# Pairs of heads on alternating halves of the array, zero-padded rotary keys, and a scaling moved to GpSimd, in the attentions of a two-block kernel

## The chip, the cores and the metric

The kernel runs on one core of a Trainium2 chip, as one launch. The metric is the device time of the launch in microseconds (us), here the median of several runs. Engine names are those of the profile: PE is TensorE's matmul side and PEld its weight load, DVE is VectorE, ACT is ScalarE, POOL is GpSimd, SP is SyncE, which issues the DMAs.

## What is computed

A token matrix x of 256 rows and 1024 features goes through two blocks of two layers each. The first block (feed-forward, a three-branch mixer, attention to a memory, feed-forward) is left alone by the change. The second block works on x and on a context of 256 more rows. Its layer 0 ("even") has two attentions side by side, a differential and a latent one, for x and for the context; its layer 1 ("odd") has one attention of 16 heads for x alone. Cut to these:

```python
def diff_attend(q, k, v, lam, lam_init, out_g):      # 4 heads, each with two 64-wide q/k parts i
    s = jnp.einsum('bhiqd,bhikd->bhiqk', q, k) * (DA_DK ** -0.5)
    p = softmax_f32(s)
    a = p[:, :, 0] - lam * p[:, :, 1]
    o = jnp.einsum('bhqk,bhkd->bhqd', a.astype(v.dtype), v)
    return rms_norm_2(o, out_g) * (1.0 - lam_init)

def mla_attend(qn, qr, kn, kr, v):                   # 4 heads: 128 plain + 64 rotary, kr shared
    s = (jnp.einsum('bhqd,bhkd->bhqk', qn, kn) + jnp.einsum('bhqd,bkd->bhqk', qr, kr)) * ((MLA_NOPE + MLA_ROPE) ** -0.5)
    p = softmax_f32(s)
    return jnp.einsum('bhqk,bhkd->bhqd', p.astype(v.dtype), v)

def na_latent(q, k, v, kc, vc, rpb):                 # 16 heads of 64, keys of x and of the context
...
        s_loc = jnp.einsum('bhqd,bhiwd->bhqiw', q_row, kb).astype(jnp.float32) * scale + bias
...
        p = softmax_f32(jnp.concatenate([s_loc, s_ctx], axis=-1))
...
```

## The kernel before, in words

Weight products, most of the program, go in three float32r passes (L241 to L243), their weights split on ACT (L236) and DVE (L237). A scheduler sets each engine's order from the traced program, the tile pools and the dependencies. Scores take a bank of the PSUM pool pj (four banks); transposes and values take one of the pool pa (four).

**Even layer.** `even_project` makes the operands; `latent_block` is called four times (two streams, two token blocks) and leaves the rotary keys `krT` on 128 rows. For each of the four heads the same 64 rotary keys serve, so both halves of the 128 rows hold them. `attend` runs units (a head and a token block of 128 queries) as a pipeline by `skew`: the scores and softmax of a unit, then its transposes (L316, copy L1309), then its values, each a stage behind the other. In `latent_attend` a unit's scores are, for each of one or two key streams, a product over 128 rows (L1239) and one over 64 rows (L1240) on the half `b` of the head. In `diff_attend` a unit has two score banks, part i = 0 on rows 0 to 63 and i = 1 on rows 64 to 127, one after the other (L1276). The context's attentions (eight units each) have 256 keys, x's have 512. Adaln weight products (L924) fill in at `fill`.

**Odd layer.** `odd_attend` has 32 units, one head h and one token block tb each. A unit: two score products over 64 rows (L1369), the bias added in PSUM on DVE (L1372), row maximum (L496), its negative (L497), the exponential with its sum on ACT (L499), the reciprocal (L501), the scaling of the 128x512 weights on DVE (L506), four transposes (L316), their copy on ACT (L1382), four value products into 64 columns of the head pair's bank (L1392). After a pair's last unit the pair's 128x256 output is split (L236, L237). The bias of a head comes from a table loaded by two DMAs from `rpbF` into a k2 tile and added to a mask on POOL (L1364), once per head. The k2 pool has seven tiles; a load waits for the tile's last reader.

The softmax's statistics `mx` and `sm` come from rings of four tiles. `fill("odd")` has nothing left to trace, as the adaln filler has ended before.

Of the kernel before, what the change touches and what calls it, by code (L numbers as in the profile page):

```python
# [35 lines left out]
# The steps take y = s y0 to 8192 s^27 v^-0.5; the seed is the negative, by its sign bit.  # L36
# [4 lines left out]
# Units of filler by the place where they are traced, a digit for each visit of it.  # L41
# [8 lines left out]
class Split:  # L50
    """Feature-major activations [128, n, 256], as an exact sum of two float32r parts."""
# [11 lines left out]
    def put(self, net, i, c, y):  # L63
        """Columns c of the features 4 i to 4 i + 3."""
        net.split(self.hs[i][:, :, c], self.ls[i][:, :, c], y)


class Joint:
    """Two streams' Splits of 1024 features in common tiles, for products with both at once."""
# [13 lines left out]
class Stream:  # L83
    """One stream of a Joint, as a Split."""
# [17 lines left out]
class Weights:  # L102
    """One loaded unit of weights as float32r parts, held in two tiles."""
# [11 lines left out]
class Net:  # L115
# [19 lines left out]
    # ---------------------------------------------------------------- tiles  # L135
# [37 lines left out]
    # -------------------------------------------------------------- weights  # L173
    def weight(self, src, n, amid=None):
        half = n // 2 if n > UNIT // 2 else n
        parts = []
        for o in range(0, n, half):
# [9 lines left out]
            if amid:  # L187
                # the first of all: by quarters, what it is for between them
# [35 lines left out]
    def fill(self, place):  # L224
        """Trace as much of the filler as belongs to this visit of a place."""
# [3 lines left out]
    def until(self, thirds):  # L229
        """Bring the adaln filler past that many thirds, and on to where it holds no bank."""  # L230
# [14 lines left out]
    def colsA(self, ps, w, base, step, xs):  # L245
        """ps [cols, 256] = (weight columns)^T x over the 1024 features."""
# [5 lines left out]
    def pair(self, src, xs):  # L252
        """Two column tiles of 128 in one bank."""
# [6 lines left out]
    def groupB(self, src, width, streams, major=False, between=None, fill=None):  # L260
        """Token-major projections of 1024 features: (stream, token block, bank) in turn."""
# [106 lines left out]
    def post_ln(self, acc, x, scale, l, i, eps, want_xs=True):  # L368
        """x = LN(scale * x + acc), in place, for the four accumulators acc[tb][nh]."""
# [15 lines left out]
    # ------------------------------------------------------------------ ffn  # L385
# [1246 lines left out]
```

## Time and profile before

| | |
|---|---|
| median of 3 runs | 2645.27 us (2642.64 to 2647.34) |
| span of the profiled execution | 2638.9 us |
| PE busy | 2581.5 us, 98% |
| DVE busy | 1495.0 us, 57% |
| ACT busy | 1176.3 us, 45% |
| POOL busy | 43.2 us, 2% |
| share of PE in the chain that ended last | 87% |
| even attentions, first L1239 to last L1253 | 1646.0 to 1767.4 us |
| odd attention, first L1369 to last L1392 | 2324.5 to 2411.6 us |

The span runs from the first to the last instruction of the profiled execution; the time of a run is taken from outside and holds a little more. "Busy" is the time in which an engine executes; the two last rows of the table are stretches of the same span, read from the timeline.

### The profile page before, as it was taken

The page shows a single profiled execution, that of the slowest core. Times are in us where ns is not written, and L with a number is a line of the kernel's source. Part 1 is how long each engine was busy: PE and PEld are TensorE (multiplying, and loading weights), DVE is VectorE, ACT ScalarE, POOL GpSimd, SP SyncE. Part 2 cuts the span into 40 slices and gives each one's busy share as a digit, 9 for nine tenths or more (in the row PEclk, how much of TensorE's full clock was granted, in tenths as well). Part 3 has the DMA queues.
Part 4 walks back from the last instruction along what each step waited for, and adds up shares of the span by engine and source line. Part 5 has one row for each costly group of instructions (what it writes and reads, how often), then busy time and mean ns, then how long its engine had stood idle before and what let it go on. Part 6 is the DMA issues. An engine that isn't in the chain of part 4 may idle for free.

```text
span 2638.9 us, 40347 instructions
## 1 busy us (share of the span) xinstructions
PE 2581.5 (98%) x15946; PEld 2178.1 (83%) x15946; DVE 1495.0 (57%) x3006; ACT 1176.3 (45%) x1953; POOL 43.2 (2%) x52
## 2 busy tenths in 40 slices
PE   8999999999999999999999999999999999999999
PEld 7997789969979978799699776567888776777997
DVE  5546765665456557655664757656222337555554
ACT  5444454554444444544544545444222325444443
POOL 0000100000000001000000000000000000010000
PEclk9999999999999999999999999899999999999999
DMA  7565335655556555256565542424222435432453
GB/s 256 189 216 191 133 112 181 200 204 206 189 179 208 197 173 204 90 168 205 203 223 191 184 152 80 140 102 150 104 96 96 161 106 186 121 72 64 169 192 136
DMA packets 136493, 424.19 MB, mean 161 GB/s; under 512 B 29752, under 2 KB 32480, under 8 KB 136304
## 3 DMA queue, kind: packets, MB, share of 16 engines
q1 hardware_dynamic: 136304, 421.62, 47.2%
q8 instruction: 125, 2.05, 0.3%
q14 instruction: 64, 0.52, 0.1%
HBM read 417.33 MB, written 4.24 MB: 160 GB/s over the span
## 4 chain that ended last, share of the span: by engine, by line
PE 87%; DVE 5%; DMA 4%; ACT 2%; issue 1%; SPq 0%; POOL 0%; ACTq 0%; DVEq 0%; POOLq 0%
PE pj L241 17%; PE pj L242 17%; PE pj L243 17%; PE pa L242 7%; PE pa L241 7%; PE pa L243 7%; PE pa L316 3%; PE pj L924 2%; DMA wf<-in_ffn_w_inA_dram 2%; PE pa L1392 1%; DVE wl L237 1%; DMA wa<-in_mod_wB_dram 1%; PE pj L1369 1%; DMA wf<-in_mix_A_dram 1%; PE pj L1276 1%
## 5 line engine op out<-in xcount | busy, mean ns | idle before, releaser
L237 DVE TENSOR_TENSOR wl<-wf,wh 128x1024 fp32r<-128x1024 f32 (+1 forms) x652 | 785.1, 1205 | 740.2 <-ACT wh L236 735.6
L236 ACT CAST wh<-wf 128x1024 fp32r<-128x1024 f32 (+1 forms) x652 | 670.6, 1032 | 929.9 <-PE pj L242 425.9
L241 PE MATMUL pj<-k,wh 128*128 128x256 f32 (+2 forms) x2896 | 841.7, 291 | 2.1 <-ACT k L236 2.1
L242 PE MATMUL pj<-k,wh 128*128 128x256 f32 (+2 forms) x2896 | 839.9, 290 | 0.0
L243 PE MATMUL pj<-k,wl 128*128 128x256 f32 (+2 forms) x2896 | 839.8, 290 | 0.0
L241 PEld LDWEIGHTS pj<-k,wh 128*128 128x128 f32 (+1 forms) x2896 | 555.3, 192 | 17.3 <-issue 7.0
L243 PEld LDWEIGHTS pj<-k,wl 128*128 128x128 f32 (+1 forms) x2896 | 555.0, 192 | 10.7 <-issue 3.4
L242 PEld LDWEIGHTS pj<-k,wh 128*128 128x128 f32 (+1 forms) x2896 | 555.0, 192 | 10.5 <-issue 3.2
L242 PE MATMUL pa<-wl,k 128*128 128x512 f32 x688 | 274.0, 398 | 0.0
L241 PE MATMUL pa<-wh,k 128*128 128x512 f32 x688 | 272.0, 395 | 0.0
L241 PE MATMUL pj<-wh,k 128*128 128x512 f32 (+1 forms) x616 | 247.8, 404 | 12.2 <-ACT wh L236 7.0
L242 PE MATMUL pj<-wl,k 128*128 128x512 f32 (+1 forms) x616 | 247.3, 402 | 0.0
L243 PE MATMUL pa<-wh,a 128*128 128x512 f32 x560 | 218.1, 389 | 0.0
L243 PE MATMUL pj<-wh,k 128*128 128x512 f32 (+1 forms) x496 | 198.5, 401 | 0.2 <-DVE k L237 0.2
L241 PEld LDWEIGHTS pj<-wh,k 128*128 128x128 f32 x616 | 117.4, 191 | 49.2 <-issue 8.3
L241 PEld LDWEIGHTS pa<-wh,k 128*128 128x128 f32 x688 | 128.8, 187 | 33.5 <-issue 0.8
L242 PEld LDWEIGHTS pa<-wl,k 128*128 128x128 f32 x688 | 129.2, 188 | 28.6 <-issue 1.0
L242 PEld LDWEIGHTS pj<-wl,k 128*128 128x128 f32 x616 | 117.3, 190 | 29.8 <-DVE wl L237 2.3
L236 ACT CAST k<-k 128x512 fp32r<-128x512 f32 (+2 forms) x152 | 85.7, 578 | 106.3 <-PE pa L242 39.0
L243 PEld LDWEIGHTS pa<-wh,a 128*128 128x128 f32 x560 | 105.3, 188 | 25.5 <-issue 0.4
L243 PEld LDWEIGHTS pj<-wh,k 128*128 128x128 f32 x496 | 94.9, 191 | 23.5 <-DVE jc L326 2.1
L237 DVE TENSOR_TENSOR a<-k,k 128x512 fp32r<-128x512 f32 x85 | 57.8, 687 | 50.4 <-ACT k L236 50.4
(252 smaller groups left out, 2523.4 us busy)
## 6 DMA issues: line engine op xcount, KB each, us to landing
wf<-in_ffn_w_inA_dram SPq DMA_DIRECT2D x262, 512.0 KB, 3.7
wf<-in_ffn_w_outB_dram SPq DMA_DIRECT2D x132, 512.0 KB, 3.8
wf<-in_mix_A_dram SPq DMA_DIRECT2D x108, 512.0 KB, 3.7
wa<-in_mod_wB_dram SPq DMA_DIRECT2D x96, 512.0 KB, 4.2
wf<-in_w_branchA_dram SPq DMA_DIRECT2D x32, 384.0 KB, 3.2
wf<-in_od_w_dram SPq DMA_DIRECT2D x24, 512.0 KB, 4.7
wf<-in_w_mix_outB_dram SPq DMA_DIRECT2D x16, 512.0 KB, 3.9
wf<-in_w_outB_dram SPq DMA_DIRECT2D x16, 512.0 KB, 7.9
```

The costliest lines, as they stand in the source:

```text
L236: self.nc.scalar.copy(h, x)
L237: self.nc.vector.tensor_tensor(l, x, h.bitcast(F32), ALU.subtract)
L241: mm(ps, sh, mh, start=start, stop=False)
L242: mm(ps, sh, ml, start=False, stop=False)
L243: mm(ps, sl, mh, start=False, stop=stop)
L316: self.nc.tensor.transpose(ps[:, i * P:(i + 1) * P], b, self.ident)
L924: mm(ps[32 * c:32 * c + 32, :256], self.cond[:, k], w[:, c * 256:c * 256 + 256], start=k == 0, stop=k == KT - 1)
L1276: mm(ps[:, j * T:(j + 1) * T], q["dqT"][b, h, c], k["dkT"][b, h], start=True, stop=True)
L1369: mm(ps[:, j * T:(j + 1) * T], q["qT"][hp // 4][b, hp % 4, c], k["kT"][hp // 4][b, hp % 4], start=True, stop=True)
L1392: mm(po[hp][b, c], kv[n // 2]["v"][n % 2][:, h * 64:h * 64 + 64], pT[:, n * P:(n + 1) * P], start=n == 0, stop=n == 3)
```

## The change

1. `latent_block` copies the rotary keys into two 128-row matrices, rows 0 to 63 of the one and rows 64 to 127 of the other; the rest is zero from two POOL memsets per stream. The rotary product of `latent_attend` is then over all 128 rows, with the matrix of the head's parity.
2. `diff_attend` takes both banks first, and issues the two parts' products alternately.
3. `attend` has one more stage, which does nothing, between the weights and their transposes.
4. `odd_attend` has units of a pair of heads and a token block, 16 of them. The two heads' scores alternate between the halves of the rows, the value products between the halves of the columns; the weights of both heads lie in one k4 tile; the scaling is a POOL instruction; a pair's biases are issued a pair ahead; there is the same empty stage; `fill("odd")` is gone.

```diff
@@ latent_block @@
-        A.copy(o["krT"][:, c], pt[:, 384:])
+        for i in range(2):
+            b = slice(64 * i, 64 * i + 64)
+            A.copy(o["krT"][b, i, c], pt[b, 384:])
@@ even_project @@
-            lat.append({"krT": self.k1(), "qnT": self.four(), "qrT": self.k2().rearrange("p (c t) -> p c t", c=2),
+            lat.append({"krT": self.t([P, 512], "sc", 2).rearrange("p (h t) -> p h t", h=2), "qnT": self.four(), "qrT": self.k2().rearrange("p (c t) -> p c t", c=2),
+            for i in range(2):
+                self.nc.gpsimd.memset(lat[s]["krT"][64 - 64 * i:128 - 64 * i, i], 0.0)
@@ latent_attend @@
-                mm(ps[:, j * T:(j + 1) * T], q["qrT"][b, h // 2, c], k["krT"][b], start=False, stop=True)
+                mm(ps[:, j * T:(j + 1) * T], q["qrT"][:, h // 2, c], k["krT"][:, h % 2], start=False, stop=True)
@@ diff_attend @@
+            banks = [self.pj() for _ in range(2)]
+            for j, k in enumerate(kv):
+                for i in range(2):
+                    b = slice(64 * i, 64 * i + 64)
+                    mm(banks[i][:, j * T:(j + 1) * T], q["dqT"][b, h, c], k["dkT"][b, h], start=True, stop=True)
             for i in range(2):
-                b = slice(64 * i, 64 * i + 64)
-                ps = self.pj()
-                for j, k in enumerate(kv):
-                    mm(ps[:, j * T:(j + 1) * T], q["dqT"][b, h, c], k["dkT"][b, h], start=True, stop=True)
@@ attend @@
-        self.skew(units, lambda u, nb, w, v, n, _: w(*u), turned, lambda u, nb, w, v, n, p: v(*u, p),
-                  lambda *_: None, lambda u, nb, w, v, n, _: n and n(*u))
+        self.skew(units, lambda u, nb, w, v, n, _: w(*u), lambda u, nb, w, v, n, p: p, turned,
+                  lambda u, nb, w, v, n, p: v(*u, p), lambda *_: None, lambda u, nb, w, v, n, _: n and n(*u))
@@ odd_attend @@
+        def weights(hp, tb, _):
+            if hp == 0 and tb == 0:
+                biases(0)
             c = slice(tb * P, (tb + 1) * P)
-            ps = self.pj()
+            banks = [self.pj() for _ in range(2)]
             for j, k in enumerate(kv):
-                mm(ps[:, j * T:(j + 1) * T], q["qT"][hp // 4][b, hp % 4, c], k["kT"][hp // 4][b, hp % 4],
-                   start=True, stop=True)
+                for i in range(2):
+                    b = slice(64 * i, 64 * i + 64)
+                    mm(banks[i][:, j * T:(j + 1) * T], q["qT"][hp // 4][b, hp % 4, c], k["kT"][hp // 4][b, hp % 4],
+                       start=True, stop=True)
             e0 = (2 - 2 * tb) * 64
-            V.tensor_tensor(ps[:, :T], ps[:, :T], bias[h][:, e0:e0 + T], ALU.add)
-            p = self.a2()
-            sm = self.softmax(ps, [(0, 512)], 1.0, p)
-            self.scale_groups(p, [(0, 512)], sm)
-            self.fill("odd")
+            p = self.k4()
+            for i in range(2):
+                ps = banks[i]
+                V.tensor_tensor(ps[:, :T], ps[:, :T], bias[2 * hp + i][:, e0:e0 + T], ALU.add)
+                pi = p[:, i * 512:i * 512 + 512]
+                sm = self.softmax(ps, [(0, 512)], 1.0, pi)
+                nc.gpsimd.tensor_scalar(pi, pi, sm[:, 0:1], 1.0, ALU.mult, ALU.mult)
+            if tb == 0 and hp < 7:
+                biases(hp + 1)
             return p
...
+            for n in range(4):
+                for i in range(2):
+                    h = 2 * hp + i
+                    mm(po[hp][64 * i:64 * i + 64, c], kv[n // 2]["v"][n % 2][:, h * 64:h * 64 + 64],
+                       pT[i][:, n * P:(n + 1) * P], start=n == 0, stop=n == 3)
...
+        self.skew([(hp, tb) for hp in range(8) for tb in range(NT)], weights, lambda hp, tb, p: p, turned, values)
```

The diff alone doesn't show the order that results. Names below are tiles with their numbers; a left side of 64x128 or 128x256 is the shape that one product writes. On PE, in the middle of the odd attention, the order before is, for some three units of one head:

```order
L1369 MATMUL pj_23115<-k_4240_21803,k_4146_21464 128x256
L1369 MATMUL pj_23143<-k_4238_21801,k_4146_21464 128x256
L1369 MATMUL pj_23143<-k_4240_21803,k_4146_21464 128x256
L316 MATMUL pa_23103<-ident,a_4549_23065 128x128 x4
L1392 MATMUL pa_23110<-a_4553_23078,k_4385_22364 64x128
L1392 MATMUL pa_23110<-a_4553_23078,k_4386_22365 64x128
L1392 MATMUL pa_23110<-a_4553_23078,k_4387_22366 64x128
L1392 MATMUL pa_23110<-a_4553_23078,k_4388_22367 64x128
L1392 MATMUL pa_23110<-a_4561_23108,k_4385_22364 64x128
```

And now, for one unit of a pair of heads (the transposes belong to the unit two before, the values to the one three before):

```order
L1379 MATMUL pj_22854<-k_4237_21808,k_4145_21471 128x256
L1379 MATMUL pj_22855<-k_4237_21808,k_4145_21471 128x256
L1379 MATMUL pj_22854<-k_4239_21810,k_4145_21471 128x256
L1379 MATMUL pj_22855<-k_4239_21810,k_4145_21471 128x256
L316 MATMUL pa_22877<-ident,k_4465_22757 128x128 x4
L316 MATMUL pa_22884<-ident,k_4465_22757 128x128 x4
L1408 MATMUL pa_22891<-a_4487_22835,k_4385_22372 64x128
L1408 MATMUL pa_22891<-a_4489_22842,k_4385_22372 64x128
L1408 MATMUL pa_22891<-a_4487_22835,k_4386_22373 64x128
```

The products of one shape stand together now, four score products of two banks by turns, then eight transposes, then eight value products of two turned tiles (two of each `a` tile's four products are seen).

On DVE, the odd attention's steady order (a unit of tb = 1, behind the reciprocals of the unit of tb = 0):

```order
L501 RECIPROCAL sm_22909<-sm_22909 128x1
L1385 TENSOR_TENSOR pj_22957<-pj_22957,k_4483_22823 128x256
L501 RECIPROCAL sm_22917<-sm_22917 128x1
L237 TENSOR_TENSOR k_4423_22634<-pa_22891,k_4421_22632 128x256
L496 TENSOR_REDUCE mx_22965<-pj_22957 128x1
L1385 TENSOR_TENSOR pj_22958<-pj_22958,k_4485_22828 128x256
L497 TENSOR_SCALAR mx_22965<-mx_22965 128x1
L496 TENSOR_REDUCE mx_22973<-pj_22958 128x1
L497 TENSOR_SCALAR mx_22973<-mx_22973 128x1
L501 RECIPROCAL sm_22966<-sm_22966 128x1
L501 RECIPROCAL sm_22974<-sm_22974 128x1
```

The scaling is gone from this engine; each unit's first bias addition stands next to the reciprocals of the unit before, which wait for ACT's sums.

On POOL, which in this stage had only the 16 bias additions, six of them now come first (heads 0 to 5), then the scalings of units 0 and 1, and then:

```order
L1367 TENSOR_TENSOR k_4483_22823<-k_4482_22820,a_4425_22636 128x384
L1388 TENSOR_SCALAR k_4450_22710<-k_4450_22710,sm_22713 128x512
L1388 TENSOR_SCALAR k_4450_22710<-k_4450_22710,sm_22721 128x512
L1388 TENSOR_SCALAR k_4465_22757<-k_4465_22757,sm_22760 128x512
L1388 TENSOR_SCALAR k_4465_22757<-k_4465_22757,sm_22768 128x512
L1367 TENSOR_TENSOR k_4485_22828<-k_4484_22825,a_4425_22636 128x384
L1388 TENSOR_SCALAR k_4477_22803<-k_4477_22803,sm_22806 128x512
L1388 TENSOR_SCALAR k_4477_22803<-k_4477_22803,sm_22814 128x512
L1367 TENSOR_TENSOR k_4510_22926<-k_4509_22923,a_4425_22636 128x384
L1388 TENSOR_SCALAR k_4492_22860<-k_4492_22860,sm_22863 128x512
L1388 TENSOR_SCALAR k_4492_22860<-k_4492_22860,sm_22871 128x512
```

An addition (heads 6, 7 and 8 here) stands ahead of the scalings of units 2, 4 and 5; it runs on to head 15 in this way, and behind it stand the scalings of the last three units alone. Each addition waits for its table's load, and the load for a k2 tile: from head 6 on either for the addition two heads back (heads 12 and 14) or, in most cases, for a bias addition of DVE.

## Rows read from the trace of the kernel before

**Rows 1.** Head of the page: busy us of each engine, its share of the span, instructions.
```profile
PE 2581.5 (98%) x15946; PEld 2178.1 (83%) x15946; DVE 1495.0 (57%) x3006; ACT 1176.3 (45%) x1953; POOL 43.2 (2%) x52
```

**Rows 2.** Windows (us, busy by engine, granted clock, DMA): four even stages, the odd one.
```profile
1646.00:1669.00 23.00, 20.99 (x80) 12.30 (x80) 12.95 (x62) 6.43 (x17) 0.00 (x0) 0.58 0.18 58
...
1677.00:1697.00 20.00, 19.92 (x142) 10.70 (x140) 15.28 (x71) 11.51 (x43) 0.00 (x0) 1.00 0.57 199
1697.00:1732.00 35.00, 34.58 (x245) 22.44 (x238) 30.11 (x117) 17.52 (x46) 0.00 (x0) 1.00 0.38 132
1732.00:1762.00 30.00, 30.00 (x161) 19.35 (x163) 18.91 (x57) 13.54 (x33) 0.00 (x0) 1.00 0.06 22
...
2324.00:2412.00 88.00, 86.22 (x528) 63.53 (x527) 57.45 (x171) 45.10 (x107) 11.95 (x11) 0.96 0.25 41
```

**Rows 3.** Timeline of PE in x's latent attention (start, length, line).
```profile
1736.14 0.60 PE L1239 MATMUL pj<-k,k 128*128 128x256 f32 x2
...
1738.55 0.66 PE L316 MATMUL pa<-ident,k 128*128 128x128 f32 x4
1739.04 1.06 PE L1290 MATMUL pa<-k,k 128*128 128x128 f32 x8
1739.93 0.38 PE L1239 MATMUL pj<-k,k 128*128 128x256 f32 x1
```

**Rows 4.** Timeline of PE in the odd attention.
```profile
2352.94 1.14 PE L1369 MATMUL pj<-k,k 64*128 64x256 f32 x8
2354.01 0.66 PE L316 MATMUL pa<-ident,a 128*128 128x128 f32 x4
2354.60 1.09 PE L1392 MATMUL pa<-a,k 128*64 128x128 f32 x8
2355.62 0.66 PE L316 MATMUL pa<-ident,a 128*128 128x128 f32 x4
...
2359.89 1.13 PE L1369 MATMUL pj<-k,k 64*128 64x256 f32 x4
2360.94 0.43 PE L1392 MATMUL pa<-a,k 128*64 128x128 f32 x2
```

**Rows 5.** Groups by line, 2324 to 2412 us: count, busy, mean ns, idle before.
```profile
L499 ACT ACTIVATE a<-pj,mx 128x512 f32<-128x512 f32 x32 | 22.2, 692 | 7.4 <-DVE mx L497 7.4
L496 DVE TENSOR_REDUCE mx<-pj 128x1 f32<-128x512 f32 x32 | 21.7, 682 | 0.2
...
L1382 ACT COPY a<-pa 128x512 f32<-128x512 f32 x32 | 18.7, 585 | 21.9 <-PE pa L316 21.9
L506 DVE TENSOR_SCALAR a<-a,sm 128x512 f32<-128x512 f32 x32 | 16.4, 512 | 0.2
...
L1372 DVE TENSOR_TENSOR pj<-pj,k 128x256 f32<-128x256 f32 x32 | 13.4, 426 | 14.6 <-PE pj L1369 14.6
...
L499 ACT ACTIVATION_READ_ACCUMULATOR a<-pj,mx 128x1 f32 x32 | 6.4, 201 | 0.0
L501 DVE RECIPROCAL sm<-sm 128x1 f32<-128x1 f32 x32 | 5.0, 157 | 6.6 <-ACT a L499 6.6
```

**Rows 6.** Timeline of POOL in the odd attention.
```profile
2327.30 1.96 POOL L1364 TENSOR_TENSOR k<-k,a 128x384 f32<-128x384 f32 x1 [20.78 <-DVE mx L497]
2336.23 1.00 POOL L1364 TENSOR_TENSOR k<-k,a 128x384 f32<-128x384 f32 x1 [6.97 <-DMA k<-in_rpbF_dram]
...
2375.15 1.00 POOL L1364 TENSOR_TENSOR k<-k,a 128x384 f32<-128x384 f32 x1 [7.00 <-DMA k<-in_rpbF_dram]
2376.76 1.00 POOL L1364 TENSOR_TENSOR k<-k,a 128x384 f32<-128x384 f32 x1 [0.61 <-DMA k<-in_rpbF_dram]
```

**Rows 7.** Timeline of DVE beside POOL's first addition.
```profile
2327.19 1.22 DVE L237 TENSOR_TENSOR wl<-wf,wh 128x1024 fp32r<-128x1024 f32 x1
```

**Rows 8.** Windows: the clock early in the odd attention, and a less busy stretch.
```profile
2331.00:2338.00 7.00, 7.00 (x27) 5.06 (x26) 4.09 (x14) 2.05 (x5) 1.00 (x1) 0.52 0.46 104
...
2205.00:2212.00 7.00, 5.76 (x39) 3.83 (x40) 6.64 (x14) 5.10 (x11) 0.00 (x0) 1.00 0.75 244
```

More of the change, by code (lines that the diff above doesn't have):

```diff
@@ L582, in mixer @@
             A.copy(iqT[:, 2 * u:2 * u + 2], ps.rearrange("p (c t) -> p c t", c=2))
-        sc = self.t([P, 384], "sc", 2)
+        sc = self.t([P, 512], "sc", 2)[:, :384]
         for h in range(8):
@@ L598, in mixer @@
                 V.match_replace(sc[:, a:e], m8, sc[:, a:e], TAKEN)
-        sel = self.t([P, 384], "sc", 2)
+        sel = self.t([P, 512], "sc", 2)[:, :384]
         V.tensor_scalar(sel, sc, -3.3e38, NEG, ALU.is_gt, ALU.mult)
@@ L1188, in even_project @@
         lat, raws = [], []
-        for _ in streams:
-            lat.append({"krT": self.k1(), "qnT": self.four(), "qrT": self.k2().rearrange("p (c t) -> p c t", c=2),
+        for s in range(len(streams)):
+            lat.append({"krT": self.t([P, 512], "sc", 2).rearrange("p (h t) -> p h t", h=2), "qnT": self.four(), "qrT": self.k2().rearrange("p (c t) -> p c t", c=2),
                         "knT": self.four(), "mv": self.k4().rearrange("p (t h d) -> p t h d", t=NT, h=4)})
+            for i in range(2):
+                self.nc.gpsimd.memset(lat[s]["krT"][64 - 64 * i:128 - 64 * i, i], 0.0)
         for s, tb, pr in self.groupB(I["ev_lat"], 448, streams, True, fill="lat"):
@@ L1234, in weights @@
         def weights(h, tb):
-            b = slice(64 * (h % 2), 64 * (h % 2) + 64)
             c = slice(tb * P, (tb + 1) * P)
@@ L1271, in weights @@
             pe = []
+            banks = [self.pj() for _ in range(2)]
[3 more added lines that the diff above has]
+                    mm(banks[i][:, j * T:(j + 1) * T], q["dqT"][b, h, c], k["dkT"][b, h], start=True, stop=True)
             for i in range(2):
-                b = slice(64 * i, 64 * i + 64)
-                ps = self.pj()
-                for j, k in enumerate(kv):
-                    mm(ps[:, j * T:(j + 1) * T], q["dqT"][b, h, c], k["dkT"][b, h], start=True, stop=True)
                 p = both[:, i * 512:i * 512 + nk]
-                pe.append((p, self.softmax(ps, [(0, nk)], 0.125, p)))
+                pe.append((p, self.softmax(banks[i], [(0, nk)], 0.125, p)))
             self.fill("difctx" if nk == T else "difx")
@@ L1351, in odd_attend, with biases @@
         bias, po = {}, {}
-        def weights(h, tb, _):
-            hp = h // 2
-            b = slice(64 * (h % 2), 64 * (h % 2) + 64)
-            if tb == 0:
+        def biases(hp):
+            for h in (2 * hp, 2 * hp + 1):
                 raw = self.k2()[:, :384]
@@ L1371, in weights @@
             e0 = (2 - 2 * tb) * 64
-            V.tensor_tensor(ps[:, :T], ps[:, :T], bias[h][:, e0:e0 + T], ALU.add)
-            p = self.a2()
-            sm = self.softmax(ps, [(0, 512)], 1.0, p)
-            self.scale_groups(p, [(0, 512)], sm)
-            self.fill("odd")
-            return p
-        def turned(h, tb, p):
-            pt = self.transposes([p[:, n * P:(n + 1) * P] for n in range(4)])
-            pT = self.a2()
-            A.copy(pT, pt)
-            return pT
-        def values(h, tb, pT):
-            hp = h // 2
-            b = slice(64 * (h % 2), 64 * (h % 2) + 64)
+            p = self.k4()
@@ new lines, in weights, with turned @@
+            for i in range(2):
[6 more added lines that the diff above has]
+                biases(hp + 1)
+            return p
+        def turned(hp, tb, p):
+            pT = []
+            for i in range(2):
+                pt = self.transposes([p[:, i * 512 + n * P:i * 512 + (n + 1) * P] for n in range(4)])
+                pT.append(self.a2())
+                A.copy(pT[i], pt)
+            return pT
@@ L1388, in values @@
+        def values(hp, tb, pT):
             c = slice(tb * P, (tb + 1) * P)
-            if h % 2 == 0 and tb == 0:
+            if tb == 0:
                 po[hp] = self.ps()
             for n in range(4):
-                mm(po[hp][b, c], kv[n // 2]["v"][n % 2][:, h * 64:h * 64 + 64], pT[:, n * P:(n + 1) * P],
-                   start=n == 0, stop=n == 3)
-            if h % 2 == 1 and tb == 1:
+                for i in range(2):
+                    h = 2 * hp + i
+                    mm(po[hp][64 * i:64 * i + 64, c], kv[n // 2]["v"][n % 2][:, h * 64:h * 64 + 64],
+                       pT[i][:, n * P:(n + 1) * P], start=n == 0, stop=n == 3)
+            if tb == 1:
@@ L1395, in values @@
                 self.split(y.h(hp), y.l(hp), po[hp][:, :T])
-        self.skew([(h, tb) for h in range(16) for tb in range(NT)], weights, turned, values)
+        self.skew([(hp, tb) for hp in range(8) for tb in range(NT)], weights, lambda hp, tb, p: p, turned, values)
         return y
```

## The prediction, made before the changed kernel had run

> **What bounds the kernel now.** I read the page's head first, then a table of windows by stage, then PE's timeline within a stage, then the groups of the odd attention by line, then POOL. The head [rows 1] says that PE is busy for 98% of the span and GpSimd for 2%: what shortens PE's work shortens the kernel, wherever no other engine stands close behind. The windows [rows 2] show where one does. In x's latent attention (1732 to 1762) PE is full and DVE at 18.9 of 30 us. In x's differential attention (1697 to 1732) DVE has 30.1 of 35. In the odd attention PE is busy for 86.2 of 88, DVE for 57.5, ACT for 45.1. The context's latent stage (1646 to 1669) is the odd one out, at a granted clock of 0.58. The timelines then show what PE is busy with. Its full time is not all columns: a product over 64 rows beside one over 128, or the next on the same half, costs drains and loads that a start-to-start reading brings out.
>
> **Prices on PE.** All are from one start to the next. In the odd attention the four records of one unit's scores (two products of two records each) on one half took 1.05 us (2359.89 to 2360.94), while eight records that happened to alternate between the halves took 1.07 (2352.94 to 2354.01) [rows 4]. So two halves by turns cost about what one costs. Four transposes take 0.59, eight value records into one half of the columns 1.02 [rows 4]. Eight full-array records of 128 columns took 0.89 (1739.04 to 1739.93), 0.11 each [rows 3].
>
> **Rotary keys.** A unit of x's latent attention has eight score records in 2.41 us (1736.14 to 1738.55) [rows 3]. Without a change of the array's mode they are eight full-array records of 256 columns, 8 x 0.22 = 1.78. That is 0.63 a unit, 5.0 us for eight units, all on PE's path, as PE is full there. The context's units have half of it, 2.5; as that stage waits in part for others and runs at 0.58 of the clock [rows 2], I take 1.5, between 0 and 4. The four memsets run on an idle GpSimd. The four more copies cost less each than ACT's 0.59 for 512 columns [rows 5], and ACT is busy for 6 of 23 us to 17 of 35 there [rows 2]: nothing, or 2.4 without that cover.
>
> **Differential scores.** A unit of x has two parts at 1.05, which become one run of 1.07: 8.2 us of PE over eight units. But DVE's 30.1 us [rows 2] would bound next, so at most 4.9 of the 35 can go. In the order some units still come out with a part's two products together, and DVE waits for ACT's sums; I take 3, between 0 and 4.9. The context's stage has half of PE's gain, 4.1, and DVE has 15.3 of 20; I take 2, between 0 and 4.1. The empty stage moves transposes a unit later and costs nothing in a pipeline of 16 units that doesn't stop. **Even layer: 5.0 + 1.5 + 3 + 2 = 11.5 us less, between 4 and 17.**
>
> **Odd attention, by engine.** Before, a unit of one head is 1.05 + 0.59 + 1.02 = 2.66 us of PE, 85 for 32 units, which is the stage (87.1 us from the first score to the last value). A unit of a pair is now 1.07 + 1.03 (eight transposes, the second four at 0.11) + 1.02 = 3.12, 50 for 16. The 1.02 for both column halves is an inference from the row halves. DVE loses 2 x 0.51 of scaling and keeps, by rows 5, two each of bias 0.43, maximum 0.68, negative and reciprocal (0.16 for each) and half a split (0.43, as the bias): 3.07. ACT has two each of 0.69 + 0.20 and 0.59, and half a cast: 3.1 [rows 5]. So three engines stand at 3.1 a unit, and none can be full, since they wait for one another in order. DVE's order goes round in two units. Laid end to end: two biases, two maxima and a negative (2.4), two exponentials with their sums (to 4.2), reciprocal, split, maximum, bias, negative (to 6.0), two exponentials (to 7.8), reciprocal: 8.0, or 4.0 a unit. Records overlap at their ends, so it is less; between 3.12 and 4.0 I take 3.65.
>
> **GpSimd.** Scaling 128x512 there is in no row. DVE's 0.51 [rows 5] bounds it below; above, the addition that took 1.96 for 384 columns beside another engine's work [rows 6], by columns 2.6. The nearest row is the usual addition, 1.00 with two inputs for 384 columns [rows 6]; with one input fewer and more columns I take 1.0. Two scalings and one addition are then 3.0 a unit, under 3.65. GpSimd binds from 1.33. The Trainium skill (GPSIMD Engine Reference, 4.1 Engine selection) gives elementwise work on a tile to VectorE, not to GpSimd. By that rule the scaling would stay, DVE would have 4.09 a unit and the stage would be 7 us longer than my sum. The rows speak against the rule here, since DVE would be the bound and GpSimd is idle. The page's 3.1 prices a one-input loop of 512 elements at 0.77 us, by which my sum stays as it is.
>
> **Table loads.** Before, a head's addition came some 8 us behind the last: 6.97 of waiting for the load and 1.00 of work [rows 6]. It hid, as heads were added ahead. Now, from head 6 on, an addition that waits holds the scalings behind it in POOL's queue, and these hold the transposes; exponentials wait for them too, through the ring of four sums. Heads 12 and 14 can load only behind the additions of 10 and 12: 8 us for two units, 4.0 a unit, for some four units. The others wait for DVE, and their loads run side by side, as the two additions only 0.61 apart show [rows 6]. I add 1.5 us, between 0 and 3.
>
> **Sum.** First scores 1.1; 16 x 3.65 = 58.4; the clock, at 0.52 from 2331 to 2338 [rows 8], makes PE's unit 6.2 and costs 7 x (1 - 3.65/6.2) = 2.9; loads 1.5; behind the last sums two scalings, transposes, copy and values, 4.2. Together 68.1 against 87.1: 19.0 less, between 12 and 29 (units of 4.0 and 3.12). **With the even layer 30.5 us less.** The terms come from an execution with a span of 2638.9 us; its median run is 2645.3, 6.4 more, the part around the span, which doesn't change. 2645.3 - 30.5 = **2614.8 us**; this case alone spans 2599 to 2629.
>
> **Rivals.**
> - **GpSimd becomes the bound (slower).** If a scaling costs p, the stage takes 22 + 34p (16 units of 2p + 1, the last two scalings, and the rest). At 2.6 that is 110 us, 23 more than now, 2657 in all. It is slower than before by over 0.2% (5.3 us, about what a measurement of this kernel can tell from no change) from p = 2.4. For it: 1.96 at 2327.30, with DVE's split (two SBUF inputs, 1.22 us at 2327.19) beside it [rows 6, 7]. Against: the usual 1.00, and DVE's steady work in the changed stage has one input in PSUM or a single one. [...] Chance 0.04; for a price near 2 (90 us, 2637) 0.06.
> - **Loads bind.** If they don't overlap, ten heads at 8 us follow 2330, then three units and the end: some 100 us, 13 more, 2647, no change. For: 8 us per head before. Against: the pair 0.61 apart. 0.07.
> - **The clock.** With PE less dense, the lower level (1.2 of 2.4 GHz) could last through the stage: 16 x 6.2 + 5.3 = 105 us, 2652. For: 0.52 behind the stage's start, where PE had gaps. Against: PE at 5.76 of 7 us kept 1.00 [rows 8], and at half clock PE is full again. 0.05.
> - **The column halves don't overlap**, so the change does half of what it says: values 2.04, PE 4.14 a unit, 7 us more than my sum, 2622. 0.06.
>
> **How the numbers follow.** My case has 0.72. Faster: 0.72 + 0.06 + 0.06 = 0.84; same 0.07; slower 0.04 + 0.05 = 0.09. The range must hold 8 in 10: my case's 2599 to 2629, the column halves and the price near 2: 2598 to 2640.
>
> **What would show it.** Right: eight value records in about 1.02 us for two heads; a scaling of 0.8 to 1.3 us; 3.5 to 3.9 us from one unit's scores to the next; DVE and ACT at 80% or more of the odd stage; x's latent attention 25 us long with PE full. Wrong: POOL's idle time before its scalings ended by table loads or POOL full (the first two rivals), a granted clock near 0.5 in most of the stage, or value runs of 2 us. If DVE leaves x's differential attention at 35 us, the term of 3 was nothing.

## Result, and the profile after

The changed kernel takes 2607.31 us (median of 4 runs, 2600.67 to 2609.2) against 2645.38 for the kernel before on the same chip: ratio 0.9856, 95% interval 0.9837 to 0.9876. That is 38.1 us less, where 30.5 were forecast; the range of 2598 to 2640 holds it. The profiled execution is the fastest of the four: its span is 2598.8 us, 40.1 under that of before. A run takes 1.9 us more than its span (2600.67 and 2598.8), so the profiled execution of before, with a span of 2638.9, took some 2640.8 (an estimate), under the median of 2645.38 too: the stages below compare two quick executions.

The page's head of the changed kernel answers to [rows 1]. PE's busy time falls by 47 us, DVE's by 16, and POOL takes 23.5 more:

```profile
PE 2534.4 (98%) x15946; PEld 2156.3 (83%) x15946; DVE 1479.2 (57%) x2974; ACT 1175.3 (45%) x1957; POOL 66.7 (3%) x88
```

I cut both traces at the same instructions: first score product of the context's latent attention, first differential score, first latent score of x, last latent value, first odd score, last odd value. The lengths in us, worked out from the starts in PE's timeline:

| stage | before | after | difference | forecast |
|---|---|---|---|---|
| from the start to the context's latent attention | 1646.0 | 1646.8 | +0.8 | 0 |
| context's latent attention | 31.3 | 23.4 | -7.9 | -1.5 |
| differential attentions, context and x | 54.6 | 49.7 | -4.9 | -5 |
| x's latent attention, to its last value | 35.5 | 30.3 | -5.2 | -5.0 |
| from there to the first odd score | 557.1 | 558.6 | +1.5 | 0 |
| odd attention | 87.1 | 63.4 | -23.7 | -19.0 |
| from the last odd value to the end | 227.4 | 226.6 | -0.8 | 0 |

The windows of the changed kernel at these cuts (us, then busy us by engine PE, PEld, DVE, ACT, POOL, then granted clock, DMA share, GB/s); the last two are six units of the odd stage, and the five behind them:

```profile
1646.80:1670.20 23.40, 20.16 (x130) 14.67 (x130) 16.06 (x74) 9.65 (x29) 0.00 (x0) 0.89 0.31 102
1670.20:1719.80 49.60, 49.40 (x369) 31.45 (x369) 42.68 (x175) 27.32 (x85) 0.00 (x0) 1.00 0.53 171
1719.80:1750.20 30.40, 30.00 (x210) 26.88 (x209) 21.93 (x72) 17.83 (x40) 0.00 (x0) 1.00 0.21 65
2308.70:2372.10 63.40, 58.13 (x519) 43.82 (x520) 44.01 (x139) 43.08 (x105) 32.64 (x43) 0.92 0.36 57
2324.70:2343.40 18.70, 18.70 (x195) 14.41 (x193) 13.47 (x44) 13.32 (x34) 10.93 (x15) 1.00 0.45 57
2343.40:2361.50 18.10, 17.48 (x164) 12.94 (x162) 13.40 (x45) 13.69 (x36) 12.20 (x17) 1.00 0.44 67
```

Against [rows 2] two things stand out. The context's latent stage has a clock of 0.89 where 1646 to 1669 had 0.58. And the odd stage has a lower clock than before, 0.92 against 0.96, and is still 23.7 us shorter.

PE's timeline in x's latent attention shows the rotary term, against [rows 3]:

```profile
1722.90 0.60 PE L1243 MATMUL pj<-k,k 128*128 128x256 f32 x2
1723.34 0.59 PE L1244 MATMUL pj<-sc,k 128*128 128x256 f32 x2
1723.77 0.59 PE L1243 MATMUL pj<-k,k 128*128 128x256 f32 x2
1724.20 0.59 PE L1244 MATMUL pj<-sc,k 128*128 128x256 f32 x2
```

Two records follow the two before after 0.43 to 0.44 us, also where the line changes: 1.74 for a unit's scores instead of 2.41.

PE's timeline in the odd attention, against [rows 4]: from the scores of one unit to the next in the first half, then in the second:

```profile
2308.74 2.00 PE L1379 MATMUL pj<-k,k 64*128 64x256 f32 x16
2313.55 1.74 PE L1379 MATMUL pj<-k,k 64*128 64x256 f32 x4 [2.82 <-ACT k L499]
...
2324.69 1.13 PE L1379 MATMUL pj<-k,k 64*128 64x256 f32 x8
2325.76 1.09 PE L316 MATMUL pa<-ident,k 128*128 128x128 f32 x8
2326.78 1.09 PE L1408 MATMUL pa<-a,k 128*64 128x128 f32 x16
2327.80 1.14 PE L1379 MATMUL pj<-k,k 64*128 64x256 f32 x8
...
2347.22 1.14 PE L1379 MATMUL pj<-k,k 64*128 64x256 f32 x8
...
2350.33 1.52 PE L1379 MATMUL pj<-k,k 64*128 64x256 f32 x8
...
2354.00 1.30 PE L1379 MATMUL pj<-k,k 64*128 64x256 f32 x8
```

Four stretches can be read. At the start, 16 records, then an idle stretch of 2.82 us until an exponential has freed a bank. Then half clock, from 2313.9 to 2324.2, with two units of 3.73 and 7.41 us. Then six units of 3.11 us (2324.69 to 2343.36), with PE without a gap: the 1.07 + 1.02 + 1.02 of the prediction. Sixteen value records of two heads take 1.02 us, where eight of one head had taken it. Then, to 2361.45, units of 3.1 to 3.9, mean 3.62 over five.

The odd stage by line answers to [rows 5] and [rows 6]:

```profile
L1388 POOL TENSOR_SCALAR k<-k,sm 128x512 f32<-128x512 f32 x32 | 22.0, 695 | 14.0 <-DVE sm L501 9.3 <-issue 1.9 <-DMA k<-in_rpbF_dram 1.3
L499 ACT ACTIVATE k<-pj,mx 128x512 f32<-128x512 f32 x32 | 21.9, 687 | 15.2 <-DVE mx L497 14.8
...
L1367 POOL TENSOR_TENSOR k<-k,a 128x384 f32<-128x384 f32 x11 | 11.0, 999 | 32.2 <-DVE pj L1385 22.3 <-DMA k<-in_rpbF_dram 6.6 <-DVE sm L501 2.3
L501 DVE RECIPROCAL sm<-sm 128x1 f32<-128x1 f32 x32 | 5.1, 162 | 12.7 <-ACT k L499 12.4
```

A scaling on POOL takes 0.695 us, less than the 1.0 I took. The additions keep 1.00. The exponentials wait for DVE's negatives (14.8 us), and the reciprocals for the exponentials (12.4): a round between two engines, neither of them busy for more than 44.0 of 63.4 us.

### The profile page after: what moved, and what is told of

Read it like the earlier page. It is cut to its first block, busy times and chain, and to the rows that moved or that the text cites. A ratio compares the mean times of both kernels' runs of the same rounds, so it can differ in the third digit from the quotient of the medians.

```text
span 2598.8 us, 40393 instructions
## 1 busy us (share of the span) xinstructions
PE 2534.4 (98%) x15946; PEld 2156.3 (83%) x15946; DVE 1479.2 (57%) x2974; ACT 1175.3 (45%) x1957; POOL 66.7 (3%) x88
## 4 chain that ended last, share of the span: by engine, by line
PE 43%; DVE 3%; DMA 2%; ACT 1%; issue 1%; POOL 0%; SPq 0%; POOLq 0%; ACTq 0%; DVEq 0%
PE pj L241 8%; PE pj L242 8%; PE pj L243 8%; PE pa L242 4%; PE pa L241 4%; PE pa L243 4%; PE pa L316 2%; PE pj L924 1%; DMA wa<-in_mod_wB_dram 1%; DMA k<-in_rpbF_dram 1%; PE pj L1280 1%; DMA wf<-in_ffn_w_inA_dram 0%; PE pa L1295 0%; PE pj L1379 0%; PE pj L1243 0%
## 5 line engine op out<-in xcount | busy, mean ns | idle before, releaser
L241 PEld LDWEIGHTS pj<-k,wh 128*128 128x128 f32 (+1 forms) x2896 | 554.2, 191 | 18.6 <-issue 6.6
L243 PEld LDWEIGHTS pj<-wh,k 128*128 128x128 f32 x496 | 94.1, 190 | 23.3 <-DVE k L237 2.4
L316 PEld LDWEIGHTS pa<-ident,k 128*128 128x128 f32 x580 | 65.3, 143 | 50.3 <-issue 18.9
```

Source lines behind the costliest of these rows:

```text
L241: mm(ps, sh, mh, start=start, stop=False)
L243: mm(ps, sl, mh, start=False, stop=stop)
L316: self.nc.tensor.transpose(ps[:, i * P:(i + 1) * P], b, self.ident)
```

## The experiments

All times are medians; a ratio is to the kernel before, run beside. The stage lengths, of one profiled execution each, are cut as above, in the order context's latent, differential, x's latent, odd:

| run | ratio, interval | ctx lat | diff | x lat | odd |
|---|---|---|---|---|---|
| before | 1 | 31.3 | 54.6 | 35.5 | 87.1 |
| the change | 0.9856, 0.9837 to 0.9876 | 23.4 | 49.7 | 30.3 | 63.4 |
| rotary keys only | 0.9942, 0.9928 to 0.9955 | 23.9 | 54.9 | 30.9 | 86.1 |
| differential scores only | 1.0000, 0.9991 to 1.0009 | 32.2 | 54.7 | 35.5 | 87.1 |
| empty stage only (even) | 0.9972, 0.9962 to 0.9983 | 32.1 | 50.6 | 35.4 | 87.2 |
| odd attention only | 0.9908, 0.9893 to 0.9923 | 33.2 | 54.6 | 35.5 | 64.1 |
| change, scaling on DVE | 0.9868, 0.9854 to 0.9881 | 23.0 | 50.6 | 30.3 | 68.1 |
| change, scores not by turns | 0.9837, 0.9824 to 0.9851 | 23.3 | 49.7 | 30.3 | 59.0 |
| change, no empty stage (odd) | 0.9905, 0.9891 to 0.9918 | 23.4 | 50.6 | 30.3 | 79.4 |
| change, tables in a2 | 0.9845, 0.9826 to 0.9865 | 26.9 | 50.6 | 30.3 | 63.4 |
| change, values not by turns | 0.9860, 0.9841 to 0.9879 | 23.3 | 50.7 | 30.3 | 64.7 |
| not by turns, filled start | 0.9823, 0.9800 to 0.9845 | 23.7 | 49.7 | 30.3 | 60.0 |
| not by turns, tables in a2 | 0.9854, 0.9833 to 0.9876 | 26.7 | 50.6 | 30.3 | 59.2 |
| all three | 0.9830, 0.9813 to 0.9847 | 22.7 | 54.2 | 30.3 | 55.7 |

### The four parts, each alone

**Rotary keys only.**

```diff
+                self.nc.gpsimd.memset(lat[s]["krT"][64 - 64 * i:128 - 64 * i, i], 0.0)
...
-                mm(ps[:, j * T:(j + 1) * T], q["qrT"][b, h // 2, c], k["krT"][b], start=False, stop=True)
+                mm(ps[:, j * T:(j + 1) * T], q["qrT"][:, h // 2, c], k["krT"][:, h % 2], start=False, stop=True)
```

> Before plus the zero-padded rotary keys alone. Theory: the padding takes the 5.0 us of mode switches in x's latent attention and 2.5 in the context's, and, as PE's rows stand closer, the clock returns earlier in the context's latent stage (10 us at half instead of 24, some 5 us): 12 to 13 us less than before, about 2632.5. Rival: the clock's part comes from another part of the change or from chance: 7.5 us less, about 2638, with 24 us at half clock between 1641 and 1669.

2629.97 us, 16.5 less, where the theory had 12 to 13; the profiled executions lie 11.5 apart, near it. x's latent attention is 4.6 us shorter, the context's 7.4. Windows of the context's stage in this kernel, in the kernel before, and in the one with the empty stage only:

```profile
1646.90:1670.80 23.90, 20.68 (x134) 15.20 (x134) 16.03 (x74) 10.04 (x30) 0.00 (x0) 0.90 0.32 100
```
```profile
1646.00:1677.30 31.30, 29.29 (x136) 17.26 (x136) 16.23 (x74) 10.23 (x31) 0.00 (x0) 0.69 0.22 77
```
```profile
1648.90:1680.90 32.00, 30.01 (x128) 17.26 (x128) 16.24 (x74) 9.67 (x30) 0.00 (x0) 0.63 0.23 75
```

DVE does the same work in all three (16.0 to 16.2 us); the clock differs, 0.90 against 0.69 and 0.63. In every kernel it falls in the same idle stretch of PE, 4.4 us long, ahead of this stage, or within 0.6 us behind it. In the kernel before it is at half level from 1641.4 to 1658.5 and from 1661.9 to 1668.7, 24 us; in the other three kernels without the padding 27.3 us, in one piece. In all ten with the padding this fall lasts 6.8 or 10.2 us, here from 1641.2 to 1651.5; two of them (those with tables in a2 whose stage is 26.7 and 26.9 us long) have a second one of 6.8. So the stage is 31.3 to 33.2 us without this edit and 22.7 to 26.9 with it: it brings the clock back, and the theory held. Why PE's denser records would do so is not shown; the edit also moves the rotary keys to another tile pool, which no run separates from the padding.

**Differential scores only.**

```diff
+            banks = [self.pj() for _ in range(2)]
+            for j, k in enumerate(kv):
+                for i in range(2):
+                    b = slice(64 * i, 64 * i + 64)
+                    mm(banks[i][:, j * T:(j + 1) * T], q["dqT"][b, h, c], k["dkT"][b, h], start=True, stop=True)
```

> Before plus the alternating differential scores alone. Theory: this alone gives the 4.9 us by which the two differential stages together are shorter after the change, about 2640.5, and the half-clock stretches of the context's latent stage stay at 24 us. Rival: without the empty stage DVE's wait for ACT bounds the stage and nothing goes: 2645, or the clock changes here too: 2636 or less.

2646.27 against 2646.44: nothing, and 54.7 us for the stages. The rival. PE's order shows why: other engines' releases still put transposes and filler between the two parts, so that few runs of scores hold both.

**Empty stage only, in the even attentions.**

```diff
-        self.skew(units, lambda u, nb, w, v, n, _: w(*u), turned, lambda u, nb, w, v, n, p: v(*u, p),
-                  lambda *_: None, lambda u, nb, w, v, n, _: n and n(*u))
+        self.skew(units, lambda u, nb, w, v, n, _: w(*u), lambda u, nb, w, v, n, p: p, turned,
+                  lambda u, nb, w, v, n, p: v(*u, p), lambda *_: None, lambda u, nb, w, v, n, _: n and n(*u))
```

> Before plus the empty stage of the even attentions alone. Theory: it costs and gives nothing, 2645 (within 2). Rival: it is what the differential stages gained by, 3 to 5 us less.

2638.46: the rival, 4.0 us less in the differential stages, with the scores traced as before. Of the 4.0, 1.5 come back as work behind the even attentions: from there to the first odd score it is 558.6 us, as in the changed kernel, instead of 557.1. The median is 8 us less, more than the trace shows, whose execution was the slowest of its seven; where the rest lies stays open. It is no wait of PE that goes: by the windows of the differential stages PE is idle for 0.5 us before and 1.0 here. What changes is PE's order. More often both parts' scores come out as one run of eight records, in 1.07 us:

```profile
1710.05 1.14 PE L1276 MATMUL pj<-k,k 64*128 64x256 f32 x8
1711.12 0.64 PE L924 MATMUL pj<-wa,cond 128*32 128x256 f32 x8
```

Such runs of eight are six here, two in the kernel before, three with the alternating scores alone. All runs of scores in these stages, each to the start of what follows, take 20.7 us here and 22.1 before: 1.4 of the 4.0.

**Odd attention only.** The whole of part 4 of the change, on the kernel before.

> Before with the odd attention of the changed kernel alone. Theory: the odd stage is 63 to 64 us as in the changed kernel and the rest as before: 23.6 us less, about 2621.8. Rival: the odd stage's start depends on the even layer's state: over 3 us away from that.

2621.93, and 64.1 us for the stage: as expected. Within 0.7 us it doesn't depend on the even layer.

### Inside the odd attention

**Scaling on DVE.**

```diff
-                nc.gpsimd.tensor_scalar(pi, pi, sm[:, 0:1], 1.0, ALU.mult, ALU.mult)
+                V.tensor_scalar(pi, pi, sm[:, 0:1], None, ALU.mult)
```

> The changed kernel with the odd scaling back on VectorE. Theory from the trace after: DVE has room (28.2 us busy of 40 in the steady part, 2.35 a unit), two scalings of 0.5 make 3.35, close to PE's 3.11 and to the 3.34 measured, and no scaling stands behind an addition that waits for a load: 0 to 4 us slower than the changed kernel, 2607 to 2611. Rival (the prediction's reading): DVE's round of waits binds at 4.1 a unit or more: 12 us or more slower than the changed kernel, 2619 or more.

2609.69, as the theory had it, and 68.1 us in the stage, 4.7 more than with GpSimd. By the traces the move to GpSimd is worth some 5 us of the 23.7, not more: DVE had room for the work. The medians lie 2.4 us apart, and their intervals overlap. Part of the 4.7 is not the scalings' own. DVE's timeline beside POOL's in this kernel:

```profile
2348.43 0.94 DVE L1388 TENSOR_SCALAR k<-k,sm 128x512 f32<-128x512 f32 x1
...
2350.02 1.13 DVE L1388 TENSOR_SCALAR k<-k,sm 128x512 f32<-128x512 f32 x1
...
2353.67 0.48 DVE L1388 TENSOR_SCALAR k<-k,sm 128x512 f32<-128x512 f32 x1
```
```profile
2348.09 1.00 POOL L1367 TENSOR_TENSOR k<-k,a 128x384 f32<-128x384 f32 x1 [4.96 <-DMA k<-in_rpbF_dram]
2349.87 1.00 POOL L1367 TENSOR_TENSOR k<-k,a 128x384 f32<-128x384 f32 x1 [0.78 <-DMA k<-in_rpbF_dram]
```

Seven of the 32 scalings begin while an addition runs. Each of them ends 0.28 us after that addition does, and six take 0.82 to 1.23 us in place of 0.48, 3.3 us more together. Four that begin ahead of an addition, or with it, keep 0.48 or 0.49.

**Scores not by turns.**

```diff
-            for j, k in enumerate(kv):
-                for i in range(2):
+            for i in range(2):
+                for j, k in enumerate(kv):
```

> The changed kernel with the odd scores of one head behind those of the other, no longer by turns. Theory: PE bounds the stage, a unit's scores take 2.1 instead of 1.07, 4.1 a unit in place of 3.34: 12 to 13 us slower than the changed kernel, about 2620. Rival: the stage waits for DVE, ACT or the loads more than for PE: less than 6 us slower.

2602.47, and 59.0 us for the stage, 4.4 less: both theory and rival missed. A unit's eight records stay at 1.07 us (2322.74 to 2323.82), though PE's order now has a head's two products together in every unit:

```profile
2322.74 1.14 PE L1379 MATMUL pj<-k,k 64*128 64x256 f32 x8
2323.82 1.09 PE L316 MATMUL pa<-ident,k 128*128 128x128 f32 x8
```

So two heads' scores overlap when they are neighbours; turns are not needed. The 4.4 us lie in three places. The slow start, to the fifth unit's scores, takes 14.1 us instead of 16.0. PE waits twice there, together as long as the 2.82 us of the changed kernel:

```profile
2312.36 1.13 PE L1379 MATMUL pj<-k,k 64*128 64x256 f32 x4 [1.61 <-ACT k L499]
2315.49 2.07 PE L1379 MATMUL pj<-k,k 64*128 64x256 f32 x4 [1.36 <-ACT k L499]
```

Half clock lasts 6.8 us instead of 10.2. Whether the order did that is not shown: with values not by turns, below, the idle stretch is 2.82 us and the fall 6.8. The eleven units behind the start take 35.8 us instead of 36.8, and from the last unit's scores to the last value it is 9.1 instead of 10.7. In these two the order of DVE differs. The scheduler orders DVE head by head in every unit, where the changed kernel has, in units of tb = 0, both maxima ahead of both negatives. DVE's timeline of the changed kernel shows one such round:

```profile
2347.14 0.74 DVE L1385 TENSOR_TENSOR pj<-pj,k 128x256 f32<-128x256 f32 x2
2347.80 1.28 DVE L496 TENSOR_REDUCE mx<-pj 128x1 f32<-128x512 f32 x2
2348.99 0.27 DVE L497 TENSOR_SCALAR mx<-mx 128x1 f32<-128x1 f32 x2
2350.04 0.16 DVE L501 RECIPROCAL sm<-sm 128x1 f32<-128x1 f32 x1 [0.78 <-ACT k L499]
...
2354.15 0.16 DVE L501 RECIPROCAL sm<-sm 128x1 f32<-128x1 f32 x1 [0.69 <-ACT k L499]
2354.23 0.74 DVE L1385 TENSOR_TENSOR pj<-pj,k 128x256 f32<-128x256 f32 x2
```

From 2347.14 to 2354.23 it is 7.09 us for two units, 3.55 each: the round of the prediction, in the units behind the six of 3.11. That those six lived on a lead which the other engines had from the slow start fits, and is not shown; nor does any run change DVE's order alone.

**No empty stage in the odd attention.**

```diff
-        self.skew([(hp, tb) for hp in range(8) for tb in range(NT)], weights, lambda hp, tb, p: p, turned, values)
+        self.skew([(hp, tb) for hp in range(8) for tb in range(NT)], weights, turned, values)
```

> The changed kernel without the empty stage in the odd attention alone. Theory: a unit's transposes stand one unit behind its scores, 3.1 us, while bias, maximum, exponential, reciprocal and scaling of two heads take some 5 us: PE waits 1 to 2 us in each unit, 15 to 30 us slower than the changed kernel. Rival: the scheduler's order hides it: within 3 us of the changed kernel.

2620.20, 79.4 us in the stage, 16 more: as expected. Half clock for 13.7 us instead of 10.2 is part of it. Transposes wait for scalings, and break the runs of scores apart; in PE's timeline of this kernel:

```profile
2344.00 0.66 PE L316 MATMUL pa<-ident,k 128*128 128x128 f32 x4 [0.61 <-POOL k L1388]
2344.58 0.70 PE L1379 MATMUL pj<-k,k 64*128 64x256 f32 x2
2345.63 0.66 PE L316 MATMUL pa<-ident,k 128*128 128x128 f32 x4 [0.36 <-POOL k L1388]
```

**Tables in a2 tiles.**

```diff
-                raw = self.k2()[:, :384]
+                raw = self.a2()[:, :384]
```

> The changed kernel with the bias tables loaded into a2 tiles, so that a load waits less and seven k2 tiles are left for the biases. Theory: the units of 3.4 to 3.9 us after 2343 in the changed kernel come from additions that wait for loads ahead of scalings on POOL; they return to 3.11: 2 to 3 us faster than the changed kernel, about 2605. Rival: those units wait for DVE and ACT, the same time within 1 us.

2604.95, and the stage at 63.4 us as before the edit: the rival. On POOL the additions hardly wait for loads any more, and the late units still take 3.1 and 3.9 by turns (7.0 for two). With DVE's round at 7.1 the loads are hidden.

**Values not by turns.**

```diff
-            for n in range(4):
-                for i in range(2):
+            for i in range(2):
+                for n in range(4):
```

> The changed kernel with the odd values of one head behind those of the other, no longer by turns; all else and every other engine's order as there. Theory A (nearness, as the scores showed): two heads' products overlap as long as they stand next to each other, sixteen records stay near 1.02 us, and the odd stage stays at 63 to 64 us, the time within 2 us of the changed kernel. Theory B (the prediction's): only by turns do the column halves overlap: sixteen records take 1.5 to 2.0 us, PE's unit 3.6 to 4.1, the odd stage 8 to 15 us longer.

2607.94: the time of theory A with the price of theory B. PE's timeline of this kernel:

```profile
2329.63 1.58 PE L1408 MATMUL pa<-a,k 128*64 128x128 f32 x16
2331.14 1.14 PE L1379 MATMUL pj<-k,k 64*128 64x256 f32 x8
```

Sixteen records take 1.51 us instead of 1.02, and every unit behind the start 3.60. Over the eleven units that is 2.9 us more than in the changed kernel, where the last five had 3.62 by DVE's round. But the slow start took 14.9 us instead of 16.0, with half clock for 6.8 us instead of 10.2, and the end 0.4 less; so the stage loses only 1.3.

Record by record, the trace shows why turns matter here and not in the scores. The first four of the sixteen start one by one, 0.11 to 0.16 us apart. The fifth and the sixth start within 0.006 us, the next ones interleave, and the last four start one by one again. In PE's order all four products of one head, of two records each, stand ahead of the other head's four; so the second head begins beside the third product of the first. In the scores a head has two products only, and there the second head's first record starts 0.013 us after the first head's. In both, the second head begins beside the last product but one of the first, and no earlier. Whether that holds for other shapes is not shown.

**Filled start**, on the version whose scores are not by turns.

```diff
+            if hp == 0 and tb == 1:
+                junk = self.ps()
+                for _ in range(8):
+                    mm(junk[:, :P], self.ident, self.ident, start=True, stop=True)
```

> The version with odd scores not by turns (the fastest so far) with eight products of the identity, whose result nobody reads, behind the scores of the first two units, where PE stands idle for 1.6 us. They stand for no work of the reference. Theory: the idle stretch is what the clock falls for some 2 us later; with it filled, the 7 us at half clock early in the odd stage go or shorten, the odd stage is 57 us or less instead of 59.0. Rival: the later idle stretch of 1.4 us, or the even earlier history, brings the fall all the same: 59 to 60 us, at half clock for 7 us or more.

2600.52, stage 60.0: not as either theory had it. The fall of the clock moved from 2314.1 to 2328.3 and lasted 3.4 us instead of 6.8. What stood ahead of it was a new idle stretch of PE, of 1.88 us, and POOL shows its cause, the loads' rival at work: an addition that waited 3.00 us, ahead of four scalings.

```profile
2325.01 1.00 POOL L1367 TENSOR_TENSOR k<-k,a 128x384 f32<-128x384 f32 x1 [3.00 <-DMA k<-in_rpbF_dram]
2325.99 2.69 POOL L1392 TENSOR_SCALAR k<-k,sm 128x512 f32<-128x512 f32 x4
```

**Scores not by turns, tables in a2 tiles** (both edits above).

> The version with odd scores not by turns, with the bias tables loaded into a2 tiles too. There three units of that version stand at 3.7 to 4.0 us, next to additions that waited for loads or stood ahead of scalings. Theory: these go, the odd stage is 57 to 58 us instead of 59.0, 1 to 2 us faster than that version (2602.5). Rival: what holds those units is DVE's and ACT's round: 59 us, the same.

2605.99. Ten of the eleven units behind the start stand at 3.12 us, the other at 3.38, so the units of 3.7 to 4.0 did come from the loads, once DVE's order no longer bound. But the slow start took 14.8 us instead of 14.1 and the end 9.8 instead of 9.1, so the stage is 59.2. And the context's latent stage, 26.7 us long, had a second stretch at half clock (1659.2 to 1666.0), though the edits are in the odd attention; with tables in a2 alone it has one too.

**All three.**

> The version with odd scores not by turns, the filled start and the tables in a2 tiles together; the eight products of the identity stand for no work of the reference. Theory: the filled start's idle 1.9 us came from the seventh head's addition, which waited 3.0 us for its load ahead of four scalings; with the tables in a2 it goes, and with it the fall of the clock behind it: the odd stage is 55 to 57 us instead of 59 to 60, about 2597. Rival: other idle stretches early in the stage bring the fall, 59 us or more, 2600 to 2606.

The stage is 55.7 us: as expected, with 3.12 us in nearly every unit behind the start and no half clock in it. The time is 2601.77, as the rival had it. In the profiled execution PE waited 2.00 us for a load of adaln weights in the differential stages, and was at half clock from 1682.8 to 1689.6:

```profile
1680.93 0.64 PE L924 MATMUL pj<-wa,cond 128*32 128x256 f32 x8 [2.00 <-DMA wa<-in_mod_wB_dram]
```

That stage took 54.2 us, where the nine other kernels with the empty stage have 49.7 to 50.7. So this version, the one with scores not by turns alone and the one with the filled start lie at 0.982 to 0.984, and their intervals overlap each other's and the changed kernel's. That their odd stages are 3.4 to 7.7 us shorter is in the traces; that the whole is faster than the changed kernel is not settled.

## Why the prediction was right, and where its steps were not

The path was right: PE's work bounds these stages, and taking from it shortened them. By the spans the change is 40.1 us where 30.5 were forecast. The 9.6 more are 6.4 in the context's latent stage and 4.7 in the odd attention, less the 1.5 of work that moved behind the even attentions.

- **Rotary keys in x's latent attention**: 5.0 forecast, 4.6 alone and 5.2 in the change. Right.
- **Rotary keys in the context's stage**: 1.5 forecast, between 0 and 4; 7.4 alone, outside these bounds. The step priced PE's own work, 2.5 at most, and took the clock of [rows 2] as given. The stage then had half clock for 4.6 us instead of 19.3, and by an estimate, the 7.4 less the 2.5, some 5 us are the clock's. This is the largest single miss, some 6 us.
- **Differential scores**: 3 + 2 forecast, 4.9 measured. That the numbers agree is luck, since the cause is another. The alternating scores gave 0; the empty stage, which the prediction priced at nothing, gave 4.0 alone. The 0.9 between 4.0 and 4.9 is no gain of turns: of the eight kernels with both and without the 2.00 us for a load, five have 50.6 or 50.7 us and three 49.7.
- **Odd attention**: 19.0 forecast, 23.7 measured. PE's unit of 3.12 was right to 0.01. The cycle of 3.65 was that of the last five units of even pace (3.62, with a round of 7.09 for two units on DVE); the six ahead of them ran at PE's pace, which is 6 x 0.54 = 3.2 us. The loads' 1.5 came to nothing, as the stage is 63.4 us with the tables in a2 too. These two make the 4.7, and two more misses cancel by luck: the start, with the clock's 2.9, has 18.6 us to the fifth unit's scores in the sum and took 16.0, and from the last unit's scores to the last value it has 7.9 and took 10.7. The scaling's 1.0 was 0.695; by the sum neither binds. The half clock's stretch was 10.2 us long instead of 7.
- **"By turns"** as the ground of the overlap was wrong for the scores (neighbourhood is enough: 1.07 us either way) and right for the values (1.02 by turns, 1.51 not). The row that seemed to show it was misread: in PE's order of the kernel before, the eight records at 2352.94 [rows 4] are two products of one head and behind them two of another, not by turns.
- **The empty stage of the odd attention**, also left without a price, is worth 16 us there.
- **The 6.4 us "around the span"** are not that. A run takes 1.9 us more than its span; the rest is a profiled execution quicker than the median. The forecast difference doesn't hang on it.
- **The signs**: the scaling lay below the 0.8 to 1.3 us that were named, and DVE and ACT were busy for 69% and 68% of the odd stage, not for 80%.
- **The rivals**: GpSimd was no bound, at 0.695 a scaling. The column halves overlapped. The loads cost nothing that shows in the changed kernel's stage and held single units in versions with scores not by turns, and the clock fell at the start of the odd stage only, for 10.2 us; neither came near the price that would have undone the gain.

By the rule of the Trainium skill that was weighed (GPSIMD Engine Reference, 4.1 Engine selection), the scaling on VectorE would be the better place, and the sum with it was 7 us longer: 4.7 measured in the stage, 2.4 between medians whose intervals overlap. By the stage the measurement decides against the rule here, for a kernel whose DVE stands in a round and whose GpSimd is idle.

## What to carry to other kernels

Put two heads' half-array products next to each other before thinking of turns, and look in the order whether they came out so: what kept them apart here was a pipeline one stage too short, and an empty stage was worth more than the reordering. Turns were needed where a head has four products and not where it has two. Where DVE and ACT are each busy for 70% of a stage, count the round of waits in the order of the engine that goes to and fro, head by head, since the pace of the later units went with that order here. And price a change by the clock of its stage too: the padded rotary keys gave back more there than PE's own work of 2.5 us.

## What the runs showed that was not expected

- In the odd stages of the ten kernels with this part of the change, every fall of the clock had an idle stretch of PE of 1.3 to 3.7 us close to its start: half clock began between 1.4 us before the stretch's end and 2.3 us after it, and lasted 3.4, 6.8 or 10.2 us, with PE full in most of it. In the changed kernel: idle 2.82 us to 2313.55, half clock from 2313.9 to 2324.2. With the idle stretches over 1 us gone (all three edits) there was none in that stage. But such a stretch is not enough: the one of 1.56 us that ends at 1654.5 in the changed kernel has no half clock in the 4 us behind it.
- These falls move between executions. The same 2.82 us of idle PE were followed by 10.2 us of half clock in four kernels and by 6.8 in two. The four runs of the filled start took 2593.0 to 2603.76 us, with a mean granted clock of 0.994 in the fastest and 0.991 in the slowest. So a single trace settles no 2 us of a stage, and parts don't add up in the medians: the four alone give 16.5 + 0.2 + 8.0 + 24.5 = 49 us, together 38.
- VectorE's scalings, with one SBUF tensor input, slowed from 0.48 to as much as 1.23 us where they began beside GpSimd's addition. The prediction had counted a single SBUF input as speaking against that rival.
